# A two-layer trunk on one core: low-rank products as fp32 row tiles, a new order of the same loop, and a start in another sequence

## The chip, the cores and the metric

The kernel runs on one core of a Trainium2 chip. The metric is the device time of one execution in microseconds (us), less is better. The work is fp32 throughout, with an error budget that rules out a plain single-pass product: most matrix products are done as three products in the format f32r, from operands that are split into a high and a low part.

## The reference

Two layers run one after the other, over 512 prompt tokens and 32 sample tokens (8 sequences of 4). Layer 0 is an RWKV-7 time mixer, layer 1 a chunked gMLP. Cut to what matters here:

```
h  = rmsnorm(x, norm_g[0])                     # D = 1024
proj = h @ w_in                                # r, k, v (E = 2048 each), wd, ad (64 each), z (E)
xm = proj + (proj of the token before - proj) * mu        # token shift, not for z
wf = w0 + tanh(wd) @ w2                        # low rank: K = 64
decay = exp(-exp(-softplus(-wf) - 0.5))
a  = sigmoid(a0 + ad @ a2)                     # low rank: K = 64
kk = k * k_k ; kk = kk / max(|kk|, 1e-12) ; k = k * (1 + (a - 1) * k_a)
S_t = S_{t-1} diag(w_t) + (S_{t-1} (-kk_t)) (kk_t * a_t)^T + v_t k_t^T ;  y_t = S_t r_t
o  = (group_norm(y) + bonus) * silu(z)
x  = x + o @ w_out
...                                            # layer 1: gMLP, then a last rmsnorm
```

Outputs are y for prompt and samples, the last rows before the shift, the final states and layer 1's v rows.

## The kernel before

The 544 tokens lie along the free dimension in two halves of 272 (256 prompt and 16 sample tokens). `start` takes the statistics of each half of x (`stats`), scales it (`scale`), transposes it and writes it split as `hh` and `hl`. The 32 heads of layer 0 are worked on as 16 head-pairs p. Each head-pair is a period of the loop: four projections of 128 columns, in the order k, r, v, z, each of 16 units. A unit is three f32r matmuls of 128 x 272 (`mm3`, L249 to L252), eight units for each half; so a period has 64 units. Half h of a projection goes to one of two PSUM banks in turn, so the first matmul of `r_p` needs the bank that ACT empties when it copies the first half of `k_p` (`raw`, L392 and L393, in `shift`).

All other work of a head-pair is written as generators, and a table `AT` gives each of their steps a due time in units; the steps of all head-pairs are sorted by it and are then issued among the projection units. The scheduler is set to manual there for all of PE, DVE, ACT, POOL and SP: the order on each engine is the order of issue, and each engine works through its own order. A second table, `BANKS`, says which PSUM bank a step uses. The stages that matter here:

- `lora_in`, once: splits tanh(wd) and ad for the low-rank products. `lora`, per p: loads the two 64 x 128 weights `lr`, makes the high part `lrh` (ACT) and the low part `lrl` (DVE), computes `plw` and `pla` (PE, L453 and L454), takes tanh of them into `xw` and `xa`, sums `xw` along the tokens to L (a scan on DVE, L473), and writes Ep = exp(-L) and Em = exp(L) (ACT, L476 and L479).
- `kpost`, `rpost`, `gram`: scale k and r by Ep and Em and form the products of a chunk (`pge`, `pgo`, kept in GK). `lanes`: stores blocks of GK to memory (`du`), reads them back in another layout (`lu`) and inverts them in 22 steps on DVE; `merge` builds the inverse of larger blocks on PE.
- `chain`: products `pz`, copies of them to XA and W (two XA copies on DVE, L843, two on ACT, L841), products `pm` and `pn`, then the serial chain over the chunks: matmul `sb` (PE, L889), update RS (DVE, L891), and the outputs `py`.
- `tail`: group norm and gate, result `of`, stored to memory `od` by SP. `smp`: the sample tokens (`pst`, `psu`, `pso`). `flip(k)`, for nine of the periods: loads a block of x (`xr`), transposes it (`pxt`, L809 and L811), stores it.

After the loop come the output products of layer 0 (`po`, from `oh` and `ol`, which are split from the loaded `od`) and then layer 1.

Of the kernel before, what the change touches and what calls it, by code (L numbers as in the profile page):

```python
# [20 lines left out]
HT = 272  # L21
# [8 lines left out]
BANKS = {'plw0': 'wa', 'plw1': 'wa', 'pla0': 'sm', 'pla1': 'sm', 'pss': 'wa', 'pge0': 'y', 'pge1': 's', 'pgo0': 'wa', 'pgo1': 'wa', 'pbo0': 'sm', 'pbo1': 's', 'pbk0': 'wa', 'pbk1': 'wa', 'pv': 'wa', 'pat': 'sm', 'pak': 'y', 'pxt': 'wa', 'psu': 'wa', 'pm1': 'g', 'pm2': 's', 'pm3': 'wa', 'pm4': 'sm', 'ps0': 'wa', 'pit': 'wa', 'psy': 's', 'pst': 'sm', 'pso': 's', 'psm': 'wa'}  # L30
# [36 lines left out]
def build(tc, A, O, off):  # L67
# [5 lines left out]
    with ctx:  # L73
# [62 lines left out]
        with tc.tile_pool(name="st", bufs=1) as st:  # L136
# [13 lines left out]
            Q.dma_start(cst, A["consts"])  # L150
# [4 lines left out]
            raws_in[1] = load_in(1)  # L155
            r1 = st.tile([113, 128], F32, name="r1")
# [45 lines left out]
            mss = [stats(0), stats(1)]  # L202
            V.tensor_scalar(xsh, xs, mss[0][0:32, 2:3], None, op0=ALU.mult)
            scale(0)
            wts0 = halves(*raws_in.pop(0))
            for h in range(2):
                for k in range(KD):
# [10 lines left out]
                    if h == 0 and k == 4:  # L218
                        scale(1)

# [137 lines left out]
        def pcol(col, p):  # L358
            return col[:, p : p + 1]
# [49 lines left out]
        lw = lH.tile([128, 2, HT], F32R, name="lw")  # L409
        la = lH.tile([128, 2, HT], F32R, name="la")  # L410
        xl = hd("xl", "h1")

        def lora_in():
            xlc, ll = (hd(n, t)[:, cl].rearrange("p (h j) -> p h j", h=2) for n, t in (("xlc", "h3"), ("ll", "h7")))
            parts = [(slice(0, 256), xl[:, 0:512].rearrange("p (h j) -> p h j", h=2)), (slice(256, 272), xl[:, 512:544].rearrange("p (h j) -> p h j", h=2))]
            for js, src in parts:
                S.activation(xlc[e_, :, js], src[e_], AF.Tanh)
            S.activation(lw[e_], xlc[e_], AF.Copy)
            V.tensor_tensor(out=ll[e_], in0=xlc[e_], in1=lw[e_], op=ALU.subtract)
            for js, src in parts:  # L420
                S.activation(la[o_, :, js], src[o_], AF.Copy)
                V.tensor_tensor(out=ll[o_, :, js], in0=src[o_], in1=la[o_, :, js], op=ALU.subtract)
            for rs, os, x in ((e_, o_, lw), (o_, e_, la)):
                S.activation(x[os], ll[rs], AF.Copy)
            yield

        lrls = [lH.tile([128, 2, 128], F32R, name=f"lrl{i}") for i in range(2)]
        for x in lrls:
            G.memset(x[o_, 0, :].bitcast(F32), 0.0)
            G.memset(x[e_, 1, :].bitcast(F32), 0.0)  # L430

        def lora(p):

            z = Z[p]
            pb = slice(128 * p, 128 * p + 128)
            lr = lH.tile([128, 2, 128], F32, name=f"lr{p}", tag="lr", bufs=1)
            for i, n in enumerate(("rw_w2", "rw_a2")):
                w = A[n][0, :, pb]
                Q.dma_start(lr[:, i, :], bass.AP(w.tensor, w.offset, [[0, 2]] + [list(x) for x in w.ap]))
            yield  # L440
            lrh = lH.tile([128, 2, 128], F32R, name=f"lrh{p}", tag="lrh", bufs=2)
            S.activation(lrh, lr, AF.Copy)
            yield
            lrl = lrls[p % 2]
            for i, rs in enumerate((e_, o_)):
                V.tensor_tensor(out=lrl[rs, i, :], in0=lr[rs, i, :], in1=lrh[rs, i, :], op=ALU.subtract)
            yield
            xa = z["xa"] = hd(f"xa{p}", "h1")
# [7 lines left out]
            def tanh(h, ps, dp_, ds_, bcol):  # L456
                S.activation(dp_[:, 4 * h : 4 * h + 4, :], ps[h][:, 0:256].rearrange("p (c j) -> p c j", j=64), AF.Tanh, bias=bcol, scale=0.5)
                S.activation(ds_[:, 4 * h : 4 * h + 4, :], ps[h][:, 256:272].rearrange("p (c j) -> p c j", j=4), AF.Tanh, bias=bcol, scale=0.5)

            for h in range(2):  # L460
                down(h, 0, lw, pw)
                yield
                tanh(h, pw, pv(xw), sv(xw), pcol(w0h, p))
                yield
                down(h, 1, la, pa)
                yield
                tanh(h, pa, cpv(xa), csv(xa), pcol(w0h, 16 + p))
                yield
# [16 lines left out]
        def kpost(p):  # L485
# [3 lines left out]
            k, xa, Ep, Em = z["k"], z["xa"], z["Ep"], z["Em"]  # L489
# [4 lines left out]
            V.tensor_tensor(out=AR[:, 0], in0=cpv(u), in1=pe(Ep), op=ALU.mult)  # L494
            yield
            AS = z["AS"] = lH.tile([128, 2, 32], F32, name=f"AS{p}", tag="AS", bufs=2)
            V.tensor_tensor(out=b4(AS[:, 0, :]), in0=csv(u), in1=se(Ep), op=ALU.mult)
# [51 lines left out]
        def rpost(p):  # L549
            z = Z[p]  # L550
            AR, AS, Ep, k2, r = (z[n] for n in ("AR", "AS", "Ep", "k2", "r"))
# [5 lines left out]
            V.scalar_tensor_tensor(out=rk2[:, cl], in0=r[:, cl], scalar=pcol(RK, p), in1=k2[:, cl], op0=ALU.mult, op1=ALU.mult)  # L557
# [169 lines left out]
        def merge(p):  # L727
# [24 lines left out]
            V.tensor_copy(right(p)[:, :, 64:128], pk.rearrange("p (j k) -> p j k", k=64))  # L752
# [69 lines left out]
        def chain(p):  # L822
# [184 lines left out]
        def tail(p):  # L1007
# [67 lines left out]
            lin=(9.80119,),
            kpost=(19.9275, 21.9207, 23.6166, 23.9847, 23.9847, 23.9847, 28.9781, 28.9781, 30.0807, 30.4572, 49.3099),
            norms=(29.8797, 29.8797, 31.3932, 43.1277, 43.3032, 43.3032),
            norms0=(27.863, 27.863, 31.1422, 33.3135, 41.7292, 52.9902),
            rpost=(34.7435, 38.6104, 38.7431, 62.3877),
            gram=(39.0376, 39.0376, 39.0376, 39.0376, 39.0376, 40.2945, 44.0649, 44.5579, 47.5737),  # L1080
            vpost=(59.4074,),
            bonus=(55.0395, 55.0395, 79.713, 79.713, 79.713, 79.713),
            gate=(56.0183, 62.5071, 67.3682, 67.3682, 67.3682, 95.5987),
            keys=(34.7135, 35.9672, 46.791, 57.01),
            sides=(73.8815, 76.9425, 82.4769, 90.6529, 90.874),
            lora=(-53.3437, -35.604, -22.0198, -6.51455, -6.51455, -5.67349, 1.68797, 1.68797, 5.54808, 5.54808, 6.00962, 7.83685, 9.52597, 14.6652, 14.6652, 18.0281),
            lora0=(-149.921, -5.42802, 0.549203, 12.1394, 12.1394, 13.3241, 13.3241, 13.3241, 13.3241, 13.3241, 13.3241, 13.3241, 13.9962, 17.1233, 17.6081, 33.6543),
            lanes=(39.112, 59.2551, 59.2551, 59.4273, 61.5138, 61.6685, 62.9447, 62.9447, 62.9447, 62.9447, 62.9447, 69.5511, 69.8722, 69.8722, 69.8722, 70.0168, 70.0168, 70.2336, 70.9978, 71.1188, 74.7254, 74.7254),
            merge=(80.6858, 90.1492, 90.1492, 91.3358, 93.8559, 94.4782, 95.4232, 98.4293, 102.797, 103.005, 103.005),
# [450 lines left out]
```

## Time and profile before

| | us |
|---|---|
| median of three runs | 1311.3 (1308.73 to 1313.69) |
| the profiled execution's own time | 1309.46 |
| its span | 1307.7 |
| PE busy in the span | 1266.9 |
| DVE busy | 991.5 |
| ACT busy | 678.4 |
| POOL busy | 158.4 |

The span is the time from the first to the last instruction of the profiled execution; what lies around it is 1.8 us. The mean granted clock of TensorE over the span is 0.993. Busy shares are means over stages with different limits.

### The profile page before, as it was taken

The numbers are of one execution on the slowest core, as the hardware profiler recorded it, in microseconds if no ns is written. First come the engines' busy times: TensorE is split into PE (matmuls) and PEld (weight loads), VectorE is DVE, ScalarE is ACT, GpSimd is POOL, SyncE is SP. The second block draws the span as 40 slices with busy tenths as digits, with TensorE's granted clock in tenths as the row PEclk, the third lists the DMA queues.
The fourth block names the chain that finished last, engine by engine and source line by source line (L and its number), as shares of the span: only waits on it lengthen the run. The fifth ranks groups of instructions, "written<-read, shape, count | busy, mean of one in ns | idle before, by whom it ended". The sixth has DMA issues, their size and how long they took to land.

```text
span 1307.7 us, 35973 instructions
## 1 busy us (share of the span) xinstructions
PE 1266.9 (97%) x14860; PEld 1207.7 (92%) x14860; DVE 991.5 (76%) x2314; ACT 678.4 (52%) x1583; POOL 158.4 (12%) x350
## 2 busy tenths in 40 slices
PE   6989999999999999999999889999999999999997
PEld 5989999999999998999989779999999999999997
DVE  5779999999999998999989877374448656556466
ACT  5666576656766765666666453253333323233333
POOL 1112121121212111221212100000000000000000
PEclk9989999999999999999999999999999999999999
DMA  4424243434434342433323464433222232231511
GB/s 155 120 59 102 68 110 97 101 89 107 102 77 112 86 108 78 109 81 91 83 69 97 115 177 115 118 98 88 81 81 83 64 106 76 61 115 53 161 36 70
DMA packets 279785, 124.31 MB, mean 95 GB/s; under 512 B 114643, under 2 KB 272485, under 8 KB 279621
## 3 DMA queue, kind: packets, MB, share of 16 engines
q1 hardware_dynamic: 259972, 106.93, 30.5%
q10 hardware_dynamic: 19648, 15.08, 3.9%
q8 instruction: 117, 1.92, 0.6%
q14 instruction: 48, 0.39, 0.1%
HBM read 102.02 MB, written 19.95 MB: 93 GB/s over the span
## 4 chain that ended last, share of the span: by engine, by line
PE 71%; DVE 16%; ACT 6%; issue 3%; DMA 2%; POOL 2%; DVEq 0%; SPq 0%; POOLq 0%; ACTq 0%
PE r_p L250 3%; PE gz_p L250 3%; PE r_p L251 3%; PE r_p L252 3%; PE gz_p L252 2%; PE gu_p L250 2%; PE gz_p L251 2%; PE gu_p L252 2%; PE gu_p L251 2%; PE gv_p L251 2%; PE gv_p L252 2%; PE gv_p L250 2%; PE pgo L580 2%; PE po L250 2%; PE po L252 2%
## 5 line engine op out<-in xcount | busy, mean ns | idle before, releaser
L250 PE MATMUL r_p<-hh,r_h 128*128 128x272 f32 x256 | 79.4, 310 | 8.8 <-ACT raw L393 8.8
L395 POOL COPY shl<-raw 128x9 f32<-128x9 f32 x49 | 27.0, 552 | 497.8 <-ACT raw L393 487.8
L250 PE MATMUL z_p<-hh,z_h 128*128 128x272 f32 x256 | 80.3, 314 | 0.0
L250 PE MATMUL v_p<-hh,v_h 128*128 128x272 f32 x256 | 79.9, 312 | 0.0
L250 PE MATMUL k_p<-hh,k_h 128*128 128x272 f32 x256 | 77.6, 303 | 0.0
L250 PE MATMUL gv_p<-hh,gv_h 128*128 128x272 f32 x256 | 75.6, 295 | 0.0
L250 PE MATMUL gz_p<-hh,gz_h 128*128 128x272 f32 x256 | 75.5, 295 | 0.0
L251 PE MATMUL r_p<-hl,r_h 128*128 128x272 f32 x256 | 74.8, 292 | 0.0
L252 PE MATMUL r_p<-hh,r_l 128*128 128x272 f32 x256 | 74.7, 292 | 0.0
L252 PE MATMUL v_p<-hh,v_l 128*128 128x272 f32 x256 | 74.4, 291 | 0.0
L251 PE MATMUL v_p<-hl,v_h 128*128 128x272 f32 x256 | 74.3, 290 | 0.0
L250 PE MATMUL gu_p<-hh,gu_h 128*128 128x272 f32 x256 | 74.2, 290 | 0.0
L251 PE MATMUL gv_p<-hl,gv_h 128*128 128x272 f32 x256 | 74.2, 290 | 0.0
L252 PE MATMUL gv_p<-hh,gv_l 128*128 128x272 f32 x256 | 74.1, 289 | 0.0
L252 PE MATMUL k_p<-hh,k_l 128*128 128x272 f32 x256 | 74.0, 289 | 0.0
L251 PE MATMUL gu_p<-hl,gu_h 128*128 128x272 f32 x256 | 73.9, 289 | 0.0
L252 PE MATMUL gu_p<-hh,gu_l 128*128 128x272 f32 x256 | 73.9, 289 | 0.0
L252 PE MATMUL gz_p<-hh,gz_l 128*128 128x272 f32 x256 | 73.9, 289 | 0.0
L252 PE MATMUL z_p<-hh,z_l 128*128 128x272 f32 x256 | 73.8, 288 | 0.0
L251 PE MATMUL gz_p<-hl,gz_h 128*128 128x272 f32 x256 | 73.7, 288 | 0.0
L251 PE MATMUL k_p<-hl,k_h 128*128 128x272 f32 x256 | 73.7, 288 | 0.0
L251 PE MATMUL z_p<-hl,z_h 128*128 128x272 f32 x256 | 73.6, 288 | 0.0
(441 smaller groups left out, 4729.4 us busy)
## 6 DMA issues: line engine op xcount, KB each, us to landing
k_r<-rw_in SPq DMA_DIRECT2D x16, 512.0 KB
r_r<-rw_in SPq DMA_DIRECT2D x16, 512.0 KB
v_r<-rw_in SPq DMA_DIRECT2D x16, 512.0 KB
z_r<-rw_in SPq DMA_DIRECT2D x16, 512.0 KB
gv_r<-gm_in SPq DMA_DIRECT2D x16, 512.0 KB
gu_r<-gm_in SPq DMA_DIRECT2D x16, 512.0 KB
gz_r<-gm_in SPq DMA_DIRECT2D x16, 512.0 KB
go_r<-gm_out SPq DMA_DIRECT2D x24, 256.0 KB
```

The source lines that it names most:

```text
L250: T.matmul(ps, whi, ahi, start=first, stop=False)
L251: T.matmul(ps, whi, alo, start=False, stop=False)
L252: T.matmul(ps, wlo, ahi, start=False, stop=last)
L395: G.tensor_copy(shl[:, :, f], raw[:, 512:553:5])
L580: T.matmul(pg[h][:, 128 * j : 128 * j + 128], BK[rs, c].rearrange("p a b -> p (a b)"), AR[rs, :, c, :], start=True, stop=True)
```

## The change

The low-rank weights are no longer split: one tile `lr` of 128 x 128 holds w2 in its upper and a2 in its lower 64 rows, and for each half two fp32 matmuls with K=64, one on each half of the rows, write two banks. `lora_in` and the f32r copies `lrh` and `lrl` go. Two copies move from DVE to ACT (ZR in `merge`, two of XA in `chain`). In `start` the columns of the identity are loaded ahead of the other constants, the statistics of the second half follow the scaling of the first, and the second scaling and the split of the first weights move inside the transposes. The tables `AT` and `BANKS` have new numbers; the order of all five engines in the loop follows from the first. Where a name is read later (`z["xa"]`, `z["Ep"]`) no instruction changes.

```
-            Q.dma_start(cst, A["consts"])
+            Q.dma_start(cst[:, 0:128], A["consts"][:, 0:128])
...
+            Q.dma_start(cst[:, 128:], A["consts"][:, 128:])
...
-            mss = [stats(0), stats(1)]
+            mss = [stats(0)]
             V.tensor_scalar(xsh, xs, mss[0][0:32, 2:3], None, op0=ALU.mult)
             scale(0)
-            wts0 = halves(*raws_in.pop(0))
+            mss.append(stats(1))
...
-                    if h == 0 and k == 4:
+                    if h == 0 and k == 2:
                         scale(1)
+                    if h == 0 and k == 6:
+                        wts0 = halves(*raws_in.pop(0))
...
-            S.activation(lrh, lr, AF.Copy)
...
-                V.tensor_tensor(out=lrl[rs, i, :], in0=lr[rs, i, :], in1=lrh[rs, i, :], op=ALU.subtract)
...
-                T.matmul(ps[h], lrh[:, i, :], x[:, h, :], start=True, stop=False)
-                T.matmul(ps[h], lrl[:, i, :], x[:, h, :], start=False, stop=True)
...
+            lr = lH.tile([128, 128], F32, name=f"lr{p}", tag="lr", bufs=2)
+            for n, rs in (("rw_w2", e_), ("rw_a2", o_)):
+                Q.dma_start(lr[rs], A[n][0, :, 128 * p : 128 * p + 128])
...
+                for x, rs in zip(ps, rw_):
+                    T.matmul(x, lr[rs], lx[rs, h, :], start=True, stop=True)
...
-            V.tensor_copy(right(p)[:, :, 64:128], pk.rearrange("p (j k) -> p j k", k=64))
+            S.activation(right(p)[:, :, 64:128], pk.rearrange("p (j k) -> p j k", k=64), AF.Copy)
...
-                        V.tensor_copy(XA[rs, h::2, :], c128(pz[a])[hs, :, 0:64])
+                    S.activation(XA[rs, h::2, :], c128(pz[a])[hs, :, 0:64], AF.Copy)
...
-            sk=(14.7847, 15.8601, 16.324, 16.6354, 16.6354, 16.6354, 16.6354),
+            sk=(0.789221, 8.8031, 15.711, 15.8424, 17.6719, 17.7726, 18.4403),
...
-            flip=(101.356, 103.429, 109.739, 165.658),
+            flip=(115.408, 135.41, 142.071, 165.144),
```

The second and third number of `sk` are the copies of the two halves of `k_p`; in `lora` the steps Ep and Em were both due at 14.6652 and are now due at 19.5291, and the scan goes from 9.52597 to 8.84795. `flip` has its load first, then its transposes.

ACT, at the start of a period in the middle of the loop (`raw` is the copy of `k_p`, Ep and Em belong to the same head-pair), before:

```order
L960 ACTIVATE GR_9068<-psm_8975,cst 128x64
L664 ACTIVATE W_9027<-pv_9028 64x4x128
L476 ACTIVATE Ep_9081<-L_9017 128x560
L479 ACTIVATE Em_9083<-L_9017 128x560
L392 ACTIVATE raw_287<-k_p 128x256
L393 ACTIVATE raw_287<-k_p 128x4x4
L369 ACTIVATE v_h<-v_r 128x1024
L392 ACTIVATE raw_287<-k_p 128x256
```

and with the change:

```order
L968 ACTIVATE so_8926<-pso_8842 128x512
L395 ACTIVATE raw_288<-k_p 128x256
L396 ACTIVATE raw_288<-k_p 128x4x4
L635 ACTIVATE W_8916<-pv_8917 64x4x128 x2
...
L395 ACTIVATE raw_288<-k_p 128x256
L396 ACTIVATE raw_288<-k_p 128x4x4
L402 ACTIVATE t_27_8999<-raw_288,prm_82 128x552
L917 ACTIVATE BT_8975<-psm_8966 128x128
L919 ACTIVATE V_8976<-psm_8966,cst 128x64
L446 ACTIVATE Ep_9015<-L_8930 128x560
L449 ACTIVATE Em_9017<-L_8930 128x560
```

The copy of the first half of `k_p` moves from behind Ep and Em to well ahead of them.

PE, at the low-rank products of the first head-pair, before:

```order
L453 MATMUL plw_467<-lw,lrh_376 128x272
L454 MATMUL plw_467<-lw,lrl_321 128x272
L250 MATMUL k_p<-hh,k_h 128x272
L251 MATMUL k_p<-hl,k_h 128x272
L252 MATMUL k_p<-hh,k_l 128x272
L453 MATMUL pla_480<-la,lrh_376 128x272
L454 MATMUL pla_480<-la,lrl_321 128x272
L453 MATMUL plw_485<-lw,lrh_376 128x272
L454 MATMUL plw_485<-lw,lrl_321 128x272
```

and with the change:

```order
L255 MATMUL k_p<-hh,k_l 128x272
L431 MATMUL plw_448<-lx,lr_323 128x272
L431 MATMUL pla_449<-lx,lr_323 128x272
L431 MATMUL plw_457<-lx,lr_323 128x272
L431 MATMUL pla_458<-lx,lr_323 128x272
L253 MATMUL k_p<-hh,k_h 128x272
```

Eight f32r matmuls become four fp32 ones, which stand in pairs.

SP, the loads and stores around `du` and `lu` of a period (`dn` and `ln` belong to the norms), before:

```order
L542 DMA ln_7053<-dn_6858 64x16
L588 DMA du_308<-GK_6906 64x4x64 x4
L112 DMA r_r<-rw_in 128x8x128
L1062 DMA od<-of_7042 128x544
L591 DMA lu_7139<-du_308 64x16x16
```

and with the change:

```order
L513 DMA ln_6943<-dn_6940 64x16
L1030 DMA od<-of_6853 128x544
L559 DMA du_309<-GK_6861 64x4x64 x4
L771 DMA xr_0_7063<-x_prompt 128x4x128
L562 DMA lu_7090<-du_309 64x16x16
L112 DMA r_r<-rw_in 128x8x128
```

The store of `od` moves ahead of the four stores of `du`.

## Rows read from the trace of the kernel before

**Rows 1.** the page: busy time of each engine, share of the span, instructions.

```profile
PE 1266.9 (97%) x14860; PEld 1207.7 (92%) x14860; DVE 991.5 (76%) x2314; ACT 678.4 (52%) x1583; POOL 158.4 (12%) x350
```

**Rows 2.** stretches: busy us (count) by engine, granted clock, DMA share, GB/s.

```profile
138.32:182.89 44.57, 44.25 (x663) 41.62 (x665) 41.05 (x104) 29.72 (x76) 9.35 (x19) 1.00 0.38 98
73.70:80.50 6.80, 5.27 (x23) 5.27 (x24) 4.71 (x9) 6.21 (x12) 1.81 (x4) 0.50 0.78 199
500.40:503.80 3.40, 3.40 (x16) 3.34 (x17) 2.05 (x6) 1.41 (x5) 0.00 (x0) 0.50 0.70 173
```

**Rows 3.** waits of PE: who for whom, us in total, times, longest.

```profile
PE r_p L250 <- ACT raw L393: 8.8, 16, 3.5
...
PE sb L889 <- DVE RS L891: 0.7, 2, 0.4
```

**Rows 4.** timeline of PE, k to r of one period: start, us.

```profile
300.49 0.28 PE L615 MATMUL pbo<-rkl,bo 128*128 128x272 f32 x1
301.09 0.39 PE L250 MATMUL r_p<-hh,r_h 128*128 128x272 f32 x1 [0.32 <-ACT raw L393]
```

**Rows 5.** timeline of ACT there.

```profile
300.60 0.37 ACT L392 ACTIVATE raw<-k_p 128x256 f32<-128x256 f32 x1
```

**Rows 6.** timeline of PE inside the projection of k.

```profile
290.28 0.29 PE L453 MATMUL plw<-lw,lrh 128*128 128x272 f32 x1
290.40 0.29 PE L454 MATMUL plw<-lw,lrl 128*128 128x272 f32 x1
```

**Rows 7.** timeline of PE, first head-pair.

```profile
71.46 0.28 PE L615 MATMUL pbo<-rkl,bo 128*128 128x272 f32 x1
75.23 0.59 PE L250 MATMUL r_p<-hh,r_h 128*128 128x272 f32 x1 [3.49 <-ACT raw L393]
```

**Rows 8.** timeline of PE at the transposes of x_sample.

```profile
500.39 0.42 PE L811 MATMUL pxt<-cst,xr 32*128 32x32 f32 x2 [1.82 <-DMA xr<-x_sample]
```

**Rows 9.** timeline of PE at the row tiles of L987.

```profile
278.68 0.48 PE L987 MATMUL pst<-We,BT 64*128 64x256 f32 x1
278.68 0.48 PE L987 MATMUL psu<-We,BT 64*128 64x256 f32 x1
...
279.31 0.34 PE L864 MATMUL pn<-W,GK 128*64 128x64 f32 x4
```

**Rows 10.** timeline of PE, from f32r into row-tiled fp32.

```profile
277.44 0.29 PE L252 MATMUL v_p<-hh,v_l 128*128 128x272 f32 x1
277.65 0.70 PE L858 MATMUL pm<-GK,XA 64*64 64x128 f32 x16
```

**Rows 11.** timeline of PE at the first low-rank products.

```profile
36.00 0.39 PE L453 MATMUL plw<-lw,lrh 128*128 128x272 f32 x1 [0.21 <-DVE ll L422]
...
38.13 0.39 PE L453 MATMUL pla<-la,lrh 128*128 128x272 f32 x1 [0.54 <-ACT xa L458]
...
40.28 0.39 PE L250 MATMUL r_p<-hh,r_h 128*128 128x272 f32 x1 [0.89 <-ACT raw L393]
```

**Rows 12.** timeline of DVE at the start.

```profile
12.20 0.50 DVE L217 SCALAR_TENSOR_TENSOR hl<-pth,ng,hh 128x272 fp32r<-128x272 f32 x1 [1.44 <-ACT hh L216]
...
14.03 1.28 DVE L191 BATCH_NORM_STATS2 bs<-xt 128x6 f32<-128x512 f32 x2
```

**Rows 13.** timeline of PE at the end of the loop.

```profile
747.07 0.59 PE L251 MATMUL po<-ol,o_h 128*128 128x272 f32 x1 [2.81 <-DVE ol L1148]
```

**Rows 14.** groups by line, 273.41 to 362.57: busy us, mean ns.

```profile
L843 DVE COPY XA<-pz 64x256 f32<-64x256 f32 x4 | 1.7, 417 | 0.2
```

**Rows 15.** timeline of SP, loads of lu.

```profile
58.03 0.60 SPq L591 DMA_DIRECT2D lu<-du  x1
...
281.01 0.60 SPq L591 DMA_DIRECT2D lu<-du  x1
```

**Rows 16.** timeline of DVE where lu is read.

```profile
61.72 0.42 DVE L682 TENSOR_TENSOR lu<-lu,ln 64x256 f32<-64x256 f32 x1 [1.29 <-DMA lu<-du]
...
286.06 0.41 DVE L682 TENSOR_TENSOR lu<-lu,ln 64x256 f32<-64x256 f32 x1
```

More of the change, by code (lines that the diff above doesn't have):

```diff
@@ L26 @@
 NORM_EPS = 1e-6
-BANKS = {'plw0': 'wa', 'plw1': 'wa', 'pla0': 'sm', 'pla1': 'sm', 'pss': 'wa', 'pge0': 'y', 'pge1': 's', 'pgo0': 'wa', 'pgo1': 'wa', 'pbo0': 'sm', 'pbo1': 's', 'pbk0': 'wa', 'pbk1': 'wa', 'pv': 'wa', 'pat': 'sm', 'pak': 'y', 'pxt': 'wa', 'psu': 'wa', 'pm1': 'g', 'pm2': 's', 'pm3': 'wa', 'pm4': 'sm', 'ps0': 'wa', 'pit': 'wa', 'psy': 's', 'pst': 'sm', 'pso': 's', 'psm': 'wa'}
+BANKS = {'plw0': 'wa', 'plw1': 'g', 'pla0': 'sm', 'pla1': 's', 'pss': 'g', 'pge0': 'g', 'pge1': 'wa', 'pgo0': 's', 'pgo1': 'wa', 'pbo0': 's', 'pbo1': 'g', 'pbk0': 'g', 'pbk1': 's', 'pv': 'y', 'pat': 'wa', 'pak': 'sm', 'pxt': 'sm', 'psu': 'wa', 'pm1': 'y', 'pm2': 'wa', 'pm3': 'sm', 'pm4': 'sm', 'ps0': 'wa', 'pit': 'wa', 'psy': 'sm', 'pst': 's', 'pso': 'wa', 'psm': 'y'}
 def _consts():
@@ L406, in shift @@
             V.scalar_tensor_tensor(out=csv(d), in0=smp[:, :, 1:5], scalar=om, in1=t1s[:, :, 0:4], op0=ALU.mult, op1=ALU.add)
-        lw = lH.tile([128, 2, HT], F32R, name="lw")
-        la = lH.tile([128, 2, HT], F32R, name="la")
+        lx = lH.tile([128, 2, HT], F32, name="lx")
         xl = hd("xl", "h1")
         def lora_in():
[L414 to L424, printed above, removed]
+            for js, src in ((slice(0, 256), xl[:, 0:512].rearrange("p (h j) -> p h j", h=2)), (slice(256, 272), xl[:, 512:544].rearrange("p (h j) -> p h j", h=2))):
+                S.activation(lx[e_, :, js], src[e_], AF.Tanh)
+                S.activation(lx[o_, :, js], src[o_], AF.Copy)
@@ L460, in lora @@
+            lr = lH.tile([128, 128], F32, name=f"lr{p}", tag="lr", bufs=2)
+            for n, rs in (("rw_w2", e_), ("rw_a2", o_)):
+                Q.dma_start(lr[rs], A[n][0, :, 128 * p : 128 * p + 128])
+            yield
             for h in range(2):
-                down(h, 0, lw, pw)
+                ps = [bk(f"pl{n}{h}", p)[:, 0:HT] for n in "wa"]
+                for x, rs in zip(ps, rw_):
+                    T.matmul(x, lr[rs], lx[rs, h, :], start=True, stop=True)
                 yield
-                tanh(h, pw, pv(xw), sv(xw), pcol(w0h, p))
@@ L464, in lora @@
[L464 to L468, printed above, removed]
+                if h == 0:
+                    xa = z["xa"] = hd(f"xa{p}", "h1")
+                for x, dp_, ds_, bcol in ((ps[0], pv(xw), sv(xw), pcol(w0h, p)), (ps[1], cpv(xa), csv(xa), pcol(w0h, 16 + p))):
+                    S.activation(dp_[:, 4 * h : 4 * h + 4, :], x[:, 0:256].rearrange("p (c j) -> p c j", j=64), AF.Tanh, bias=bcol, scale=0.5)
+                    S.activation(ds_[:, 4 * h : 4 * h + 4, :], x[:, 256:272].rearrange("p (c j) -> p c j", j=4), AF.Tanh, bias=bcol, scale=0.5)
+                    yield
@@ L493, in kpost @@
             AR = z["AR"] = l0.tile([128, 2, NCH, 64], F32, name=f"AR{p}", tag="AR", bufs=2)
-            V.tensor_tensor(out=AR[:, 0], in0=cpv(u), in1=pe(Ep), op=ALU.mult)
+            V.tensor_tensor(out=AR[:, 0], in0=cpv(u), in1=pe(z["Ep"]), op=ALU.mult)
             yield
             AS = z["AS"] = lH.tile([128, 2, 32], F32, name=f"AS{p}", tag="AS", bufs=2)
-            V.tensor_tensor(out=b4(AS[:, 0, :]), in0=csv(u), in1=se(Ep), op=ALU.mult)
+            V.tensor_tensor(out=b4(AS[:, 0, :]), in0=csv(u), in1=se(z["Ep"]), op=ALU.mult)
             yield
@@ L502, in kpost @@
             ua = hd(f"ua{p}", "h7")
-            V.scalar_tensor_tensor(out=ua[:, cl], in0=xa[:, cl], scalar=1.0, in1=u[:, cl], op0=ALU.add, op1=ALU.mult)
+            V.scalar_tensor_tensor(out=ua[:, cl], in0=z["xa"][:, cl], scalar=1.0, in1=u[:, cl], op0=ALU.add, op1=ALU.mult)
             yield
             k2 = z["k2"] = hd(f"k2_{p}", "h8")
-            S.activation(k2[:, cl], xa[:, cl], AF.Identity, scale=pcol(kah, p), bias=pcol(ka1, p))
+            S.activation(k2[:, cl], z["xa"][:, cl], AF.Identity, scale=pcol(kah, p), bias=pcol(ka1, p))
             yield
@@ L550, in rpost @@
             z = Z[p]
-            AR, AS, Ep, k2, r = (z[n] for n in ("AR", "AS", "Ep", "k2", "r"))
+            AR, AS, Ep, r = (z[n] for n in ("AR", "AS", "Ep", "r"))
             V.tensor_tensor(out=AR[:, 1], in0=cpv(r), in1=pv(Ep), op=ALU.mult)
@@ L556, in rpost @@
             rk2 = z["rk2"] = hd(f"rk2{p}", "h1")
-            V.scalar_tensor_tensor(out=rk2[:, cl], in0=r[:, cl], scalar=pcol(RK, p), in1=k2[:, cl], op0=ALU.mult, op1=ALU.mult)
+            V.scalar_tensor_tensor(out=rk2[:, cl], in0=r[:, cl], scalar=pcol(RK, p), in1=z["k2"][:, cl], op0=ALU.mult, op1=ALU.mult)
             yield
@@ L1075, in build @@
[L1075 to L1087, printed above, removed]
@@ L1091, in build @@
-            chain=(103.35, 103.492, 104.192, 104.192, 104.45, 104.45, 104.45, 106.129, 107.734, 110.12, 110.344, 110.344, 110.344, 110.344, 110.983, 110.983, 111.461, 111.99, 111.99, 116.223, 116.571, 118.245, 119.291, 120.662, 122.737, 122.737, 123.448, 124.261, 126.451, 128.474, 134.567, 137.125, 137.125, 137.16, 138.698, 138.698, 151.352, 196.182),
-            tail=(137.741, 139.93, 141.783, 143.235, 143.593, 146.755, 149.322, 152.651, 159.432, 160.601, 160.601, 163.12, 163.738, 163.738, 166.987, 169.754, 174.977, 174.977),
@@ L1093, in build @@
-            flip=(101.356, 103.429, 109.739, 165.658),
+            wk=(-24.6703, -13.9502, -10.5009),
+            wr=(-1.92923, 4.85448, 5.61825),
+            wv=(0.606097, 15.3323, 15.3323),
+            wz=(26.5557, 37.8471, 43.6636),
+            sk=(0.789221, 8.8031, 15.711, 15.8424, 17.6719, 17.7726, 18.4403),
+            sr=(7.54549, 28.6206, 31.674, 31.674, 34.0009, 34.0009, 38.5955),
+            sv=(43.7782, 45.1654, 47.4232, 49.7307, 49.7307, 51.0746, 55.203),
+            sl=(-48.6951, -2.31874, 1.08412, 4.68622, 4.68622, 4.68622, 4.68622),
@@ new lines, in build @@
+            lin=(5.21945,),
+            kpost=(24.9494, 25.986, 25.986, 25.986, 26.4478, 26.4478, 26.4478, 28.1479, 28.7234, 28.9758, 46.1589),
+            norms=(26.5963, 27.2646, 42.3595, 42.3595, 43.7228, 43.7228),
+            norms0=(30.3638, 36.1029, 36.1029, 42.7321, 43.0652, 43.81),
+            rpost=(34.2118, 40.034, 43.0665, 59.6417),
+            gram=(38.5207, 38.5207, 38.5207, 38.5207, 38.5507, 38.7256, 44.4019, 46.8335, 55.0017),
+            vpost=(57.36,),
+            bonus=(47.1621, 50.0087, 67.1245, 68.9711, 69.0871, 71.7472),
@@ new lines, in build @@
+            gate=(58.7304, 58.7304, 68.9911, 70.1851, 70.432, 104.018),
+            keys=(51.7578, 52.1495, 90.6263, 93.0718),
+            sides=(71.9966, 73.0768, 73.0768, 79.7128, 89.332),
+            lora=(-37.6497, -16.243, -12.6778, -6.32377, -6.32377, -5.15096, 0.12609, 0.958916, 8.84795, 19.5291, 19.5291, 39.8259),
+            lora0=(-48.6977, 9.64576, 9.64576, 9.68669, 9.68669, 9.68669, 9.68669, 9.68669, 9.69389, 18.8347, 22.6537, 30.7022),
+            lanes=(4.59191, 56.0959, 56.1972, 56.1972, 57.7957, 57.8272, 57.8272, 59.1798, 61.4444, 61.4444, 61.7838, 61.7838, 63.4843, 63.4843, 64.0257, 64.7786, 65.5865, 65.5865, 68.1234, 68.1534, 76.599, 78.8691),
@@ L1094, in build @@
+            tail=(132.502, 132.502, 132.572, 132.98, 132.98, 141.147, 141.337, 146.854, 147.433, 159.083, 159.098, 163.745, 164.046, 166.048, 166.166, 166.34, 168.968, 171.692),
+            flip=(115.408, 135.41, 142.071, 165.144),
         )
```

40 lines of the change are left out of this document (5 added, 35 removed).

## The prediction

> **What bounds the kernel now.** I read the page first: TensorE is busy 97% of the span [rows 1]. Then one plain period of the first layer's loop: in 44.57 us PE is busy 44.25, DVE 41.05 and ACT 29.72 [rows 2], so the loop is paced by PE, and DVE is near enough behind to matter. Then the chain of waits on PE, since time can only come from PE's instruction stream getting shorter or from PE's waits. The largest wait is one kind: `r_p` waits 8.8 us in 16 places for ACT's evacuation `raw` of `k_p` [rows 3]. The timeline shows it as a pattern: `pbo` starts at 300.49, `r_p` only at 301.09 [rows 4], because ACT starts that evacuation at 300.60 [rows 5], right behind Em in its order. A plain step is 0.125 us (290.28 to 290.40 [rows 6]), so 0.476 is lost, and about 0.10 more, as the first matmul after an idle stretch runs 0.39 instead of 0.28 us. That comes in 14 periods. The same wait is 3.49 us at 75.23 [rows 7]. Afterwards the granted clock is the lower of its two levels: from 73.70 to 80.50 it is 0.50, with 23 matmul rows [rows 2]. From 75.23 to 80.50 are 5.27 us, and 23 plain steps would be 2.9, so the stall also costs 2.4 us of clock. A second long stall is 1.82 us at 500.39, until the load of `x_sample` lands [rows 8], with half clock from 500.40 to 503.80 [rows 2]: 3.40 us of busy PE, of which 1.5 are due to the clock.
>
> **The low-rank products.** Per period eight f32r matmuls go: 8 x 0.125 = 1.00 us (the pair in [rows 6] shows two of them). Two pairs of fp32 row tiles come. The kernel has one such operation already: `pst`/`psu`, K=64, 128 columns out, two instructions on two row halves; both start at 278.68 and the next group at 279.31 [rows 9], 0.63 us for 256 columns, so 0.67 for 272, and 1.34 for two pairs. Bounds: not under 0.25 for a pair (two f32r steps), not over 1.36 (nothing side by side: 0.67 twice); I take the row of the same form. That row stands between tiled groups. Going from f32r into a row-tiled group costs 0.21 in place of 0.125 (277.44 to 277.65 [rows 10]). In the order of after one more such entry stands in a period (4 for 3) and one return to f32r from fp32 fewer (13 for 14): these cancel, by +0.09 and -0.085. Net +0.34 us per period, 15 periods: +5.1.
>
> A rule speaks against the change here. The row that bears on it is the 0.21 at 277.65 [rows 10]. The Trainium skill, TensorEngine Tiling (Array Packing), section Key Properties, states that changing the tiling mode drains TensorE. Charged at both sides of both pairs it would be 4 x 0.09 x 16 = 5.8 us on top by the row's excess, an estimate, in place of one entry. I keep the smaller count, since the order puts the first pair right behind the tiled `pn`.
>
> DVE loses the two subtractions, ACT the copy `lrh`; these are off PE's path and enter the sum at nothing while DVE and ACT are below PE [rows 2]. SP still issues two loads of `lr`, of half the bytes.
>
> **The evacuation of k, per period.** The order of ACT has `raw_k` ahead of Ep and Em instead of behind. The first half's copy is due at unit 8.8 of 64, when its eight units have been issued, and not at 15.9; the period is 44.57 us, so a unit is 0.70 and the copy has some 5 us before r_p needs its bank. What was late, Ep and Em, goes from unit 14.7 to 19.5, 3.4 us later; its readers (AR, BK of `kpost`) go from about unit 20 to 25, so with them. So 14 x 0.58 = -8.1. New small waits: the orders of after, followed with the durations of before, leave slacks of 0.1 to 0.4 us in places (`sb` behind `ND`, `pyt` behind the norm, bank g behind the tanhs). I charge 0.1 per period: +1.5. Ends: 0 and 0.8 (a rival).
>
> **The start of the loop.** The 3.49 us: there L, Ep, Em and raw stand behind the 22 steps of `lanes`; in after raw_k stands ahead of them. PE gains 3.6 (71.46 to 75.23 was 3.77, a step 0.125) and the 2.4 of clock: -6.0, ends -6.0 and 0. `lora_in` shrinks to four ACT instructions: its waits are 0.21, 0.54 and 0.89 of idle at 36.00, 38.13 and 40.28 [rows 11], together 1.64, with some 0.15 for each restart: -2.1, ends -2.5 and 0.
>
> **Start.** The second half's statistics now stand ahead of the first `hl`. DVE sat idle 1.44 us before the first `hl` at 12.20, and the two statistics rows take 1.28 [rows 12], so they fit. The weights' halves move from before k=0 to k=6, so `lora_h` on ACT starts later, by up to one pass over such a tile, ahead of the first product; such a pass is near the 1.28 of that row. I take half of it less what the earlier scaling gives back: +0.5, ends -1 and +2. Loading the identity alone gives nothing that I can see: the first transposes wait for xsh.
>
> **The flip.** The load xr is issued at unit 115.4 and transposed at 135.4, 20 units or 14 us apart, against 2 units before. The 1.82 stall with its clock goes: -3.3, ends -3.3 and 0. The `sb` waits of 0.7 in 2 places [rows 3] came from DVE standing at rkl until an od store was done; with od earlier I take -0.7, ends -0.7 and 0.
>
> **Tail.** PE waits 2.81 us for the third `ol` at 747.07 [rows 13]. In after py and pso stand ahead of that row, but the operands come about as early: I take -1.5, ends 0 and -5 with the clock after it.
>
> **XA and ZR copies to ACT, DVE's queue.** Two XA copies of 0.417 us [rows 14] leave DVE, and two more stand ahead of W's copies on ACT. I charge nothing more than the 0.1 above, as DVE loses more work than ACT gains.
>
> **Sum.** +0.5 - 2.1 - 6.0 - 3.3 - 0.7 - 1.5 in the places outside the periods = -13.1; periods +5.1 - 8.1 + 1.5 = -1.5; together -14.6. The profiled run of before took 1309.46 us, 1.84 under the median 1311.3; from the profiled run it is 1294.9, from the median 1296.7. I say **1296**.
>
> **The rivals.**
> B, the row tiles do not run side by side: two pairs cost 1.36 each instead of 0.67, +1.38 x 15 = +20.7: 1317. Against it: `pst` and `psu` start at the same time [rows 9]. Chance 0.06.
> C, ACT paces the state chain: the two XA copies now wait in one queue with W's copies, 2 x 0.417 = 0.8 us later [rows 14], and pm and sb with them. Where PE has no other work in its order there, 0.8 x 15 = +12: 1308. For it: DVE and ACT feed the sb chain step by step, and PE waits there today [rows 3]; against it: between the steps stand projection matmuls. Chance 0.11.
> D, the long stall at 75 us stays: the evacuation comes early in order but p=1's operands, or another wait of that crowded stretch, still hold PE. +6.0: 1302. For it: everything there is behind `lanes`, whose chain starts with p=0's late gram. Chance 0.13.
> E, slower: SP's order. `od` of the head-pair before now stands in front of the `du` stores and `lu`, so if DVE writes its `of` late, SP holds du and lu, and DVE, which handles rows in order, waits at `lu` with the RS subtractions of the sb chain behind it. Today lu is issued at 281.01 [rows 15] and read at 286.06 [rows 16]; at p=0 DVE had it 3.69 us after the issue (58.03 [rows 15], 61.72 after an idle 1.29 [rows 16]). So a steady period has 5.05 - 3.69 = 1.36 us to spare, and in the order of after, followed the same way, 1.8 to 2.8. To end slower than before by 0.5% it must cost 14.6 + 6.6 = 21.2 us, 1.4 a period on top of that slack; so it decides from a delay of some 3.5 us on. The price would be 1318 or more. Chance 0.10.
> The likeliest case has 0.60, its own range 1289 to 1303.
>
> **How the numbers follow.** About 0.5% (6.6 us) can be told from no change: under 1304.7 is faster, over 1317.9 slower. Faster: the likeliest case but for 0.01 of it, and D: 0.72. The same: B, C and that 0.01: 0.18. Slower: E: 0.10. The range 1285 to 1310 holds the likeliest case, D and C; it leaves out B and E, 0.16, and a little of the tails. Below it reaches to -10.6 from 1296: if the periods take no new waits (-1.5), the tail goes wholly (-3.5), the start's +0.5 is -1 and the row tiles are half a step cheaper (-4).
>
> **What would show it.** Right: no idle before r_p, and `r_p` gone from PE's waits; no PE gap around 70 us and at the eighth flip, and granted clock 1.0 there; plw and pla starting at one time, the next f32r matmul 0.67 later; a plain period of 44.4 to 44.6. Wrong: a new releaser in PE's waits in 14 or so periods (W, XA or RS: C; lu or ltm: E), or a pair of over 1 us (B).

## The result and the profile after

The changed kernel takes 1303.57 us (median of five, 1301.43 to 1303.82) where before took 1311.3: a ratio of 0.9934, with the 95% interval 0.9916 to 0.9952. It is faster by 0.66%, 7.7 us, which is only a little over half of the 14.6 us that were forecast. The time lies in the range that was given (1285 to 1310), but just outside the likeliest case's own range (1289 to 1303). The profiled run took 1301.43, its span fell by 8.1 us.

The page and the chain of PE's waits of the changed kernel (who waits for whom, us in total, times, longest; two waits of the start are left out):

```profile
span 1299.6 us, 35877 instructions
...
PE 1270.6 (98%) x14860; PEld 1199.3 (92%) x14860; DVE 962.9 (74%) x2231; ACT 690.7 (53%) x1612; POOL 128.1 (10%) x346
```

```profile
...
PE po L255 <- DVE o_l L119: 2.3, 1, 2.3
PE po L254 <- DVE ol L1116: 1.8, 3, 1.4
PE pm L717 <- DVE T L707: 1.7, 1, 1.7
PE psy L943 <- ACT Zf L764: 1.2, 1, 1.2
PE pgo L551 <- DVE AR L523: 1.1, 1, 1.1
PE sb L857 <- DVE RS L853: 0.9, 1, 0.9
PE pm L826 <- ACT W L815: 0.6, 1, 0.6
...
```

Two things are to be seen beside [rows 1, 3]. The wait of `r_p` for the copy of k, 8.8 us in 16 places, is gone, and nothing of its size took its name. Yet PE is busy 3.7 us longer. The profile counts 14860 matmuls in both kernels, since each fp32 row tile is two records: the waits that went were partly filled by PE's own work becoming longer. A plain period shows it (stretch: its length, then busy us of PE, PEld, DVE, ACT, POOL, the clock, DMA share, GB/s), against the 44.57 of [rows 2]:

```profile
274.07:319.11 45.04, 44.93 (x662) 41.39 (x663) 39.25 (x98) 30.62 (x78) 6.72 (x19) 1.00 0.37 95
```

By the starts of the first `k_p` matmul of a head-pair in the two timelines, the 8 us come from few places:

| stretch | before | after | difference |
|---|---|---|---|
| start to the first k | 30.71 | 31.40 | +0.7 |
| head-pair 0 | 31.94 | 31.89 | 0.0 |
| head-pair 1 (with the stall at 75 us) | 46.59 | 43.06 | -3.5 |
| head-pairs 2 to 9 | 358.79 | 359.89 | +1.1 |
| head-pair 10 (with the load of x_sample) | 48.28 | 45.03 | -3.3 |
| head-pairs 11 to 14 | 179.52 | 179.20 | -0.3 |
| head-pair 15, to the first po | 44.04 | 44.28 | +0.2 |
| po to the first gv | 129.92 | 127.07 | -2.9 |
| the first gv to PE's last instruction | 431.28 | 431.30 | 0.0 |

Three of these differences are to be read with care. The first row is no more than what traces of the same start differ by (28.75 to 31.60 us in the runs below that keep the changed start and its order). For `po` to `gv` the traces with the new tables and an untouched tail have 125.19 to 128.70, those with the old tables 128.90 to 129.93, so the gain is there and its size is not sure. The rows of head-pairs 2 to 9 and 11 to 14 set longer plain periods against four of before (45.26, 45.26, 45.37 and 46.44 us) that held waits of `sb` and `pss`.

The plain periods, for which -0.1 each was forecast, became longer by 0.47 where nothing but the `r_p` wait had disturbed them. Where that comes from is read on PE's timeline, in pieces of the same period:

```profile
273.67 0.29 PE L255 MATMUL v_p<-hh,v_l 128*128 128x272 f32 x1
274.07 0.35 PE L826 MATMUL pm<-GK,XA 64*64 64x128 f32 x4
...
278.32 0.29 PE L255 MATMUL z_p<-hh,z_l 128*128 128x272 f32 x1
278.45 0.33 PE L857 MATMUL sb<-RS,MB 128*128 128x64 f32 x2
278.71 0.48 PE L955 MATMUL pst<-We,BT 64*128 64x256 f32 x1
...
279.34 0.43 PE L857 MATMUL sb<-RS,MB 128*128 128x64 f32 x2
279.61 0.28 PE L613 MATMUL pbk<-cst,BK 128*128 128x128 f32 x1
...
282.54 0.33 PE L857 MATMUL sb<-RS,MB 128*128 128x64 f32 x2
282.80 0.49 PE L431 MATMUL plw<-lx,lr 64*128 64x272 f32 x1
282.81 0.49 PE L431 MATMUL pla<-lx,lr 64*128 64x272 f32 x1
283.14 0.39 PE L431 MATMUL plw<-lx,lr 64*128 64x272 f32 x1
283.14 0.39 PE L431 MATMUL pla<-lx,lr 64*128 64x272 f32 x1
283.46 0.39 PE L253 MATMUL z_p<-hh,z_h 128*128 128x272 f32 x1
...
313.93 0.43 PE L943 MATMUL psy<-W,MM 128*128 128x64 f32 x2
314.30 0.56 PE L806 MATMUL pz<-ZR,Zf 64*64 64x128 f32 x12
```

At 274.07 `pm` starts 0.40 us after the matmul ahead of it; it waits for ACT's copy W, which ends just before, and this is the 0.11 us in which PE is not busy in the period. The column `64*128` is the part of the array (rows * columns) that an instruction uses. A pair starts at one time and is done after 0.66 us (282.80 to 283.46), as forecast. But `sb`, on the whole array, takes 0.26 until the row tiles after it may start (278.45 to 278.71, 282.54 to 282.80). Before it took 0.14 with f32r behind it:

```profile
283.13 0.33 PE L889 MATMUL sb<-RS,MB 128*128 128x64 f32 x2
283.27 0.37 PE L250 MATMUL z_p<-hh,z_h 128*128 128x272 f32 x1
```

An `sb` that follows row tiles takes 0.27 to the transpose behind it (279.34 to 279.61), and `psy` between two tiled groups 0.37 (313.93 to 314.30); before, it took 0.26. Over the period the 14 records of `sb` take 1.54 us, each counted to the start of the next matmul, where they took 1.03. Before, the period had 6 unbroken stretches of matmuls on a part of the array; in the changed order it has 10, because `pst`/`psu` no longer stand between `pm` and `pn`, the second pair stands alone, `psm` is apart from `py`, and `psy` cuts `pgo` from `pz`.

### The profile page after: what moved, and what is told of

Its sections match the earlier page's. It is cut to its first block, busy times and chain, and to the rows that moved or that the text cites. A ratio compares the mean times of both kernels' runs of the same rounds, so it can differ in the third digit from the quotient of the medians.

```text
span 1299.6 us, 35877 instructions
## 1 busy us (share of the span) xinstructions
PE 1270.6 (98%) x14860; PEld 1199.3 (92%) x14860; DVE 962.9 (74%) x2231; ACT 690.7 (53%) x1612; POOL 128.1 (10%) x346
## 4 chain that ended last, share of the span: by engine, by line
PE 88%; ACT 5%; DVE 3%; DMA 2%; issue 1%; SPq 0%; POOL 0%; ACTq 0%; POOLq 0%; DVEq 0%
PE z_p L253 3%; PE gz_p L253 3%; PE gz_p L255 2%; PE gu_p L253 2%; PE gz_p L254 2%; PE gu_p L255 2%; PE gu_p L254 2%; PE gv_p L254 2%; PE gv_p L255 2%; PE gv_p L253 2%; PE k_p L253 2%; PE k_p L254 2%; PE k_p L255 2%; PE r_p L253 2%; PE z_p L255 2%; PE po L253 2%
## 5 line engine op out<-in xcount | busy, mean ns | idle before, releaser
L253 PE MATMUL v_p<-hh,v_h 128*128 128x272 f32 x256 | 76.6, 299 | 0.0
L253 PEld LDWEIGHTS z_p<-hh,z_h 128*128 128x128 f32 x256 | 48.3, 189 | 10.8 <-issue 10.4
```

The source lines that it names most:

```text
L253: T.matmul(ps, whi, ahi, start=first, stop=False)
```

## The experiments

The theory: every stretch of tiled matmuls among whole-array ones costs PE time at its entry and at its leaving, and the new order with its pairs has more of them; that took back much of what the vanished waits gave. The rivals: the early copy of k is what matters and something else eats it; or the chain over ACT (pz, XA, W, pm), rival C, sets the period, so that PE's work is not the bound at all. Ratios are to the kernel before, run in the same session.

**e1: the early copy of k alone, in the kernel before.** The first four numbers of `sk`.

```
-            sk=(14.7847, 15.8601, 16.324, 16.6354, ...
+            sk=(0.789221, 8.8031, 15.711, 15.8424, ...
```

> The kernel before with one line of the table changed: the copies of k_p out of PSUM are due as in the changed kernel (units 8.8 and 15.7 instead of 15.86 and 16.3). Theory: r_p waits only for the copy of the first half, which stood behind Ep and Em. Then 14 waits of 0.58 us go (8.1 us) and the stall of 3.77 us at 71 us with its half clock goes (up to 6.0): about 1297 where before takes 1311. Rival: the wait only changes its name, since L, Ep and Em pace the same place by other readers; then 1306 to 1311. By the trace of the changed kernel, where the first period is only 3.5 us shorter, the stall at 71 us may give back about 3.5 rather than 6.0: 1299 to 1300.

Measured: 1312.86, ratio 1.0003 (0.9989 to 1.0018). The rival held. The `r_p` wait goes, and the period is 44.42 instead of 44.57, but in 14 periods `pm` now waits for another copy on ACT, `fs`, which stands behind `u`, and `u` stands still until DVE has written k:

```profile
PE pm L746 <- ACT fs L911: 4.8, 14, 0.3
...
PE plw L453 <- DVE ll L422: 2.4, 1, 2.4
```

```profile
305.16 0.75 ACT L491 ACTIVATE u<-k,prm 128x544 f32<-128x544 f32 x1 [0.34 <-DVE k L406]
305.93 0.27 ACT L911 ACTIVATE fs<-pfs 64x128 f32<-64x128 f32 x1
```

The rest went at the first low-rank products, which waited 2.4 us for the split operands (second row), and in two longer periods (46.63 and 48.99 us), where PE stood at `sb` and at `pss`, `r_p` and `pm` without a releaser that the profile shows. The line alone gave nothing here.

**e7: the late copy of k in the changed kernel.** The reverse, the first four numbers of `sk` as before.

> The changed kernel with the copies of k_p due as before (units 15.86 and 16.3). Theory: in this order, too, r_p then waits for the copy, which comes behind W, s, sq and v_h on ACT; by the rows of before 0.5 to 0.6 us in 14 or 15 periods, +7 to +9: about 1311. Rival: with Ep and Em out of the way the late copy is in time, 1303 to 1305.

Measured: 1305.13, ratio 0.9941 (0.9926 to 0.9956), which is the changed kernel's own within the intervals. The period is 45.22 instead of 45.04. So 0.18 a period is what the early copy gives here, not 0.58: with Ep and Em out of the way the late copy is nearly in time. That it was Ep and Em that held the copy up is read from ACT's order and fits this; no run moved them alone.

**e2 and e8: the flip.** In e2 the kernel before gets the new due times of `flip`, in e8 the changed kernel the old ones.

```
-            flip=(101.356, 103.429, 109.739, 165.658),
+            flip=(115.408, 135.41, 142.071, 165.144),
```

> The kernel before with the four due times of flip of the changed kernel. Theory: the stall of 1.82 us at the transposes of x_sample and the half clock after it (1.5 us) go: about 1308, and the period at 497 us falls from 48.3 to about 45. Rival: the load lands late again or the transposes collide with other work in their new place in nine periods: 1311 or more.

> The changed kernel with the due times of flip as before (101.4 and 103.4 instead of 115.4 and 135.4). Theory: the load of x_sample lands late again, so one stall of about 1.8 us with its half clock, +3; the nine blocks of x_prompt have had their load in time before. But the reverse experiment on the kernel before cost 23 us through waits of pv, so a due time that does not fit the rest of the table may cost as much here: 1306 if only the stall returns, 1315 or more if the transposes hold up others in nine periods.

Measured: e2 1336.61, ratio 1.0191 (1.0169 to 1.0214); e8 1315.1, ratio 1.0016 (1.0001 to 1.0032). Each costs something in every period with a flip: in e2 `pv` waits 21.3 us in 9 places, in e8 `pxt` waits 7.7 us in 8, and in e8 the stall on `x_sample` is back with 1.8.

```profile
PE pv L661 <- DVE m L1023: 21.3, 9, 2.6
```

```profile
PE pxt L780 <- DVE ysr L951: 7.7, 8, 1.0
...
PE pxt L782 <- DMA xr<-x_sample: 1.8, 1, 1.8
```

The first row is e2's, the two others are e8's. The rival held both times. The later flip removes the stall in both orders, as no wait for `x_sample` is left in e2 either, but in the order of before it holds up others. What exactly `pv` waits for in e2 was not taken apart.

**e11: the row tiles alone, in the kernel before.** The four low-rank steps that are gone are taken out of the table; all else is as before.

```
-                T.matmul(ps[h], lrh[:, i, :], x[:, h, :], start=True, stop=False)
-                T.matmul(ps[h], lrl[:, i, :], x[:, h, :], start=False, stop=True)
+                for x, rs in zip(ps, rw_):
+                    T.matmul(x, lr[rs], lx[rs, h, :], start=True, stop=True)
```

> The kernel before with the fp32 row tiles alone: pairs in the places of the first product of each half, the four steps less in the table, all other due times as before. By the price in the prediction (1.34 for 1.00, entries cancelling) +0.34 per period and -2 at the preparation: 1314 to 1315. By the theory that each pair standing alone among f32r matmuls costs another 0.1 to 0.2 for entering and leaving: +0.5 to +0.7 per period, 1317 to 1320. If the freed time of DVE and ACT mattered: below 1311.

Measured: 1320.1, ratio 1.0063 (1.0042 to 1.0083). The theory held, at its upper end. The period, in which PE's order differs in nothing else, is 45.26 where it was 44.57 [rows 2]:

```profile
279.93:325.19 45.26, 44.93 (x663) 41.29 (x663) 40.61 (x102) 29.42 (x75) 9.40 (x19) 1.00 0.37 95
```

```profile
287.83 0.29 PE L252 MATMUL z_p<-hh,z_l 128*128 128x272 f32 x1
288.04 0.49 PE L428 MATMUL plw<-lx,lr 64*128 64x272 f32 x1
288.05 0.49 PE L428 MATMUL pla<-lx,lr 64*128 64x272 f32 x1
288.38 0.39 PE L428 MATMUL plw<-lx,lr 64*128 64x272 f32 x1
```

Of the +0.69, two pairs for eight f32r matmuls are 1.32 - 1.00 = 0.32. The other 0.37 are two stretches more, entered at 0.21 in place of 0.125 (287.83 to 288.04) and left into an f32r matmul that is as slow to be followed as after any fp32 one: 0.18 per stretch. The leaving half is also what an f32r matmul takes behind a whole-array fp32 one (0.21, `v_p` at 312.49 in e9 below), so this run does not tell it from a change of tiling. The freed DVE and ACT time bought nothing.

**e3 and e5: the changed kernel with f32r products.** Everything as changed, but `plw` and `pla` from split weights in the places of the pairs. In e3 the copy `lrh` was due at -24, in e5 at -28.

```
-                for x, rs in zip(ps, rw_):
-                    T.matmul(x, lr[rs], lx[rs, h, :], start=True, stop=True)
+                for i, x in enumerate((lw, la)):
+                    T.matmul(ps[i], lrh[:, i, :], x[:, h, :], start=True, stop=False)
+                    T.matmul(ps[i], lrl[:, i, :], x[:, h, :], start=False, stop=True)
```

> The changed kernel with the low-rank products as before, f32r with split weights, eight matmuls of 0.125 us instead of two pairs, in the places of the pairs; everything else as changed. Theory (changes between row-tiled and whole-array matmuls cost PE time): two pairs take 1.32 us and f32r 1.00, and the second pair stands alone, so one stretch of tiled matmuls less: 0.12 to 0.15 more. In all -0.45 us per period, -7 in 15, and +2 for the longer preparation at the start: about 1298 to 1299, a period of 44.6 instead of 45.04. Rival (the extra 0.47 us per period over before comes from the new order or from ACT's longer work, not from the pairs): 1303 to 1306, as DVE and ACT get their splitting work back.

> The f32r products in the changed kernel again, with the copy lrh due 4 units earlier: in the first attempt it stood on ACT between the copies XA and W, and pm waited 0.55 us for W instead of 0.11, which hid what the products themselves are worth. Theory: now PE has 0.3 us less of products and one tiled stretch less, 0.45 in all, and the wait for W is 0.1 again: a period of 44.6 instead of 45.04, in all about 1297 to 1299. Rival: the period stays at 45.0, because not PE but the chain over pz, XA, W and pm sets it: 1303 or more, with the wait for W grown again.

Measured: e3 1306.18, ratio 0.9945 (0.9924 to 0.9965); e5 1300.19, ratio 0.9906 (0.9893 to 0.9919). In e3 the period stayed at 45.08, since `lrh` stood on ACT between the copies XA and W, and `pm` waited 0.55 for W:

```profile
274.50 0.35 PE L850 MATMUL pm<-GK,XA 64*64 64x128 f32 x4 [0.55 <-ACT W L839]
```

With `lrh` 4 units earlier (e5) the period is 44.62, as forecast from the products and one stretch less, and `pm` waits for W as in the changed kernel. Counted from start to start, the products themselves take 0.12 us less, the `z_p` matmuls 0.19 and `sb` 0.09. The first period lost 3.4 us to the longer preparation (35.34 against 31.89), so of the 6.3 us of 15 periods about 3 were left.

```profile
273.10:317.72 44.62, 44.52 (x661) 41.71 (x661) 39.64 (x101) 30.88 (x79) 6.71 (x19) 1.00 0.38 98
```

So both bounds are there, close together: PE's own work, which sets e5's period, and the chain over ACT, which takes the same 0.4 us back as soon as one more copy stands in it (e3).

**e4: the copies ZR and XA back on DVE, in the changed kernel.** The two lines of the diff undone.

> The changed kernel with the copies ZR and two of XA back on DVE. If the short wait of pm for W (0.11 us and 0.07 of restart in each period) comes from four XA copies in a row on ACT, it goes: -0.18 x 15 = -2.7, about 1301. Rival: DVE, with 1.5 us more per period, paces the sb chain and PE waits there: 1305 or more. No effect at all would be 1303 to 1304.

Measured: 1299.97, ratio 0.9903 (0.9879 to 0.9928). The total is where the first number expected it, but not for its reason: the period is 45.01, the wait for W only 0.02 shorter. What went is the stall of 1.7 us in head-pair 1, which is 41.23 instead of 43.06; but that stall is 0.9 in e9, which leaves the copies alone, so the copies need not be its cause. Moving the copies to ACT is not what makes the changed kernel faster; that it makes it slower lies within the intervals.

**e6 and e9: fewer tiled stretches, in the changed kernel.** In e6 `pst`, `psu` go behind the first pair and `psy` behind `pz`; in e9 only `psy` moves. No work changes.

```
-            102.52, 102.958, 103.396, 105.645, 115.209,
+            102.52, 103.3,   103.396, 105.645, 111.76,      # e6
+            102.52, 103.3,   103.396, 105.645, 115.209,     # e9
```

> The changed kernel with two due times of the sample stage moved, so that two stretches of row-tiled matmuls join others: pst and psu directly behind the pair plw, pla, and psy behind pz instead of between pgo and pz. No work is taken out. Theory (each entry and leaving of a tiled stretch costs about 0.1): in the trace sb before pst takes 0.205 instead of 0.084 and sb after psu 0.160 instead of 0.055, and psy costs 0.365 instead of 0.259 with another entry; so -0.2 to -0.38 us per period, a period of 44.7 to 44.85, 3 to 5.6 us in all, about 1298 to 1300. Rival (the entries only fill time in which PE would wait for sb or W): period 45.0, 1303.

> The changed kernel with one due time moved: psy behind pz instead of between pgo and pz, so that those two stretches of tiled matmuls meet. In the last attempt, which moved pst as well, pst then waited for ND, but the rows of psy and pge together fell by 0.165 us per period. Theory (entries and leavings cost): period 44.87 instead of 45.04, 2.5 us in all, about 1301. Rival (PE's next wait takes it up, for W or RS): period 45.0, 1303.

Measured: e6 1317.23, ratio 1.0039 (1.0025 to 1.0053); e9 1296.99, ratio 0.9893 (0.9872 to 0.9913). In e6 `psy` became cheaper as the theory has it, but `pst` in its new place waits for ND, with `sb` behind it:

```profile
PE pst L955 <- DVE ND L847: 13.3, 16, 2.4
...
PE sb L857 <- DVE RS L859: 6.0, 15, 0.7
```

e9 leaves that out. The period falls from 45.04 to 44.76, and PE is busy for all of it (the wait for W is gone from it):

```profile
270.92:315.68 44.76, 44.76 (x662) 41.32 (x662) 39.22 (x99) 30.60 (x78) 6.71 (x19) 1.00 0.38 96
```

```profile
312.35 0.33 PE L943 MATMUL psy<-W,MM 128*128 128x64 f32 x2
312.49 0.37 PE L253 MATMUL v_p<-hh,v_h 128*128 128x272 f32 x1
312.70 0.29 PE L254 MATMUL v_p<-hl,v_h 128*128 128x272 f32 x1
...
315.46 0.29 PE L255 MATMUL v_p<-hh,v_l 128*128 128x272 f32 x1
315.68 0.35 PE L826 MATMUL pm<-GK,XA 64*64 64x128 f32 x4
```

Per period the rows of `psy` fall from 0.365 to 0.138, those of `pge` (now followed by `pz`) rise by 0.062: 0.165 for one stretch less. Half of that is given back, since the f32r matmul now behind `psy` takes 0.21 until the next (312.49 to 312.70) in place of 0.125: 0.08 is left. The larger part of the gain is W's: `pm` starts 0.22 behind its neighbour (315.46 to 315.68) and not 0.40, so 0.18 went, since `pz` starts earlier. One number of the table is worth 4 us in 15 periods, and the interval lies wholly under that of the changed kernel: e9 beats both.

**e10: put together.** e9, with the copies back on DVE, and f32r products from the second head-pair on (the first keeps row tiles, its split operands being prepared behind its own products).

> Put together: the changed kernel with f32r low-rank products from the second head-pair on and fp32 row tiles only for the first (whose products stand behind the preparation), psy behind pz, and the ZR and XA copies back on DVE. Theory: -0.42 per period from the products (period 44.62 in the run with f32r), -0.165 from psy, and no 3.4 us lost in the first period as in that run: a period of 44.4 to 44.5, about 1292 to 1295. Rival: the preparation of the split operands, now beside the first head-pair's scan on ACT and DVE, holds up Ep and so pgo, or DVE with its added work paces sb: 1297 to 1300.

Measured: 1301.56, ratio 0.9925 (0.9903 to 0.9948): the rival. The period is 44.8, not 44.4, as `pm` waits again for W:

```profile
PE pm L865 <- ACT W L854: 2.2, 13, 0.2
```

and the first period is 34.61, though it keeps its row tiles. Which of the three changes makes W late for the shorter PE order was not taken apart. Whether f32r products with `psy` moved and XA left on ACT would do better than e9 was not tried.

**e12: the start alone, in the kernel before.** The lines of `start` from the diff.

> The kernel before with the changed start alone. The prediction has +0.5 (from -1 to +2) for it: 1311 to 1312; in the trace of the changed kernel the projection of k starts 0.7 us later than before. Rival: the earlier scaling pays, the first product starts earlier and k by 0.5 to 1 us, 1310.

Measured: 1314.04, ratio 1.0008 (0.9993 to 1.0023): no difference that can be told; the +0.5 forecast is too small to be told.

## Why the prediction was right in direction and short in size

- **The `r_p` wait.** It went in all periods, as forecast. The mechanism was half right: e7 shows that in the new order even the late copy is nearly in time, e1 that moving the copy alone only hands the wait on. The 8.1 us are about right as the sum of the waits: counted from start to start, `pbo` and `r_p` take 0.51 us less in a plain period, 7.1 in 14.
- **The price of the row tiles.** The term was "+0.34 us per period, 15 periods: +5.1", with entry and return that "cancel, by +0.09 and -0.085". The pair itself was right (0.66 against 0.67). In the new order the row tiles cost 0.42 a period against f32r in the same places (e5); in the order of before, where both pairs stand alone among f32r matmuls, 0.69 (e11). By the Trainium skill, TensorEngine Tiling (Array Packing), section Key Properties, a change of the tiling mode drains TensorE. The traces here agree at the entry: from an f32r matmul it is 0.21 us to a row tile (287.83 to 288.04 in e11) and 0.13 to a whole-array fp32 matmul (278.32 to 278.45). The prediction had the sum 4 x 0.09 per period and set it aside, because it looked only at the first pair, which stands behind `pn`; the second stands alone behind `sb`.
- **The order's own stretches: the step that failed.** The prediction counted only entries out of f32r and returns to it ("4 for 3", "13 for 14"). It put at nothing that `pst`/`psu`, `psm` and `psy` change their neighbours, though the order shows it: the count is 10 stretches for 6, and most of the new ones border on whole-array fp32 matmuls (`sb`, `psy`). The period's +0.47 comes out as -0.51 for the `r_p` wait, +0.42 for the row tiles, +0.18 for W's wait with its restart (0.40 in place of 0.22), and +0.38 that is left. In e5, with f32r products and 9 stretches, this 0.38 shows in `sb` (1.45 a period, before 1.03) and `psy` (0.365, before 0.26), while other matmuls take somewhat less; no run takes these three stretches away together. They make some 5.7 us in 15 periods, an estimate, most of the 6.9 us that are missing from the forecast; W's wait is 0.08 over the 0.1 charged for small waits. From head-pair 2 to 15 (but for 10) the loop became only 1.0 us longer, since the waits in four periods of before went: the `sb` waits of 0.7 [rows 3], as forecast, and two of `pss` that no term of the prediction had. An `sb` wait of 0.9 stands in head-pair 15 instead.
- **Head-pair 0 and 1.** Forecast -2.1 and -6.0; measured 0.0 and -3.5. The waits named did go, and the granted clock is 1.00 there: `pbo` and `r_p` of head-pair 1 take 6.0 us less, as forecast. But `pgo` now waits 1.1 us for AR, and at 78.34 `pm` waits 1.72 for T, which stands behind a load `Zf`: half of rival D, in another wait of the same crowded stretch.

```profile
78.34 0.24 PE L717 MATMUL pm<-T,GK 64*64 64x64 f32 x1 [1.72 <-DVE T L707]
```

```profile
77.49 0.71 DVE L707 STREAM_TRANSPOSE T<-Zf 128x512 f32<-128x512 f32 x1 [1.84 <-DMA Zf<-dz]
```

- **The flip.** -3.3 forecast, -3.3 measured, in part by luck: the period without the stall is also 0.47 longer, so the stall with its clock was worth 3.7. And e2 and e8 show that the later flip is a gain only with the other due times.
- **Tail and start.** -1.5 forecast, -2.9 measured; +0.5 forecast, +0.7 measured. Neither size is sure, as the spreads beside the table show.
- **The rivals.** B is out (`plw` and `pla` start together). C shows in small: 0.11 us per period, 0.55 as soon as one more copy stands in ACT's way (e3). E did not come: `lu` is in no wait of PE.

## What to carry to other kernels

Where a kernel is bound by PE and mixes matmuls on parts of the array with whole ones, count the unbroken stretches of each kind in the order, and price each at both ends: a matmul that saves no time by itself can cost twice its own excess by standing alone (0.69 for 0.32 in e11). A wait that is removed from a tuned order can move to the next in-order queue (e1), so price a table of due times as one thing and not line by line. When a new order has been found, look for single steps that cut a tiled stretch in two and can be moved by a fraction of a unit.

## What had not been expected of the hardware

The small whole-array `sb` (64 columns) takes 0.26 us to the row tiles behind it, against 0.14 to an f32r matmul; but that f32r matmul then takes 0.21 until the next, so what a stretch costs in the end is less than its own rows show (0.08 for 0.165 in e9). And the two fp32 row tiles of K=64 with 272 columns, though side by side, take 0.66 us against 0.50 for four f32r matmuls of the full array, so for a split of two terms the split is the cheaper one on PE even without the entries.
